# The context's loads, norm and modulation, moved from behind the q projections to ahead of the last GLU pair

## The chip, the cores and the metric

One core of one Trainium2 chip runs the whole program in one launch. The metric is the time of one execution on the device in microseconds; the median of several runs is compared. The core has five engines that run side by side, each with its own list of instructions that it takes in order: TensorE (matmuls, PE), VectorE (DVE), ScalarE (ACT), GpSimd (POOL) and SyncE (SP), which here issues the DMA transfers. They wait for each other by semaphores.

## The reference

The program computes two blocks on 512 tokens of width 1024, in float32. The change lies in the first, a mixer with attention and convolution that is conditioned on a vector `c` and on a context of 256 tokens:

```python
mod = silu(c) @ w_mod + b_mod;          shift, scale, gate = split(mod, 3)
mod_c = silu(c_ctx) @ w_mod + b_mod;    shift_c, scale_c, gate_c = split(mod_c, 3)
u  = rms_norm(x,   norm_w) * (1 + scale)   + shift
uc = rms_norm(ctx, norm_w) * (1 + scale_c) + shift_c
p = u @ w_in                            # columns: q, k, v, za, GLU (a and g), zc
q, k, v = heads of p; q and k rms-normed per head, then rotated by position
k_c, v_c = heads of uc @ w_in[:, k and v columns]; k_c rms-normed
attn = softmax(q @ [k_c; k].T / 8) @ [v_c; v] * silu(za)
conv = pointwise(silu(layer_norm(depthwise_conv31(a * sigmoid(g))))) * silu(zc)
h = x + gate * (concat(attn, conv) @ w_out)
```

So the context enters in one place: its normed and modulated rows `uc` are multiplied with the key and value columns, and give 256 further keys and values. The second block (a delta-rule recurrence, attention to a memory, a feed-forward layer) follows on `h` and is not touched.

## The kernel before, in words

**Numbers.** Every large matmul is done in three passes: each operand is split into a high part (a rounded copy, by ScalarE) and a low part (the difference, by VectorE), and `mm3` adds high x high, high x low and low x high. A weight slab of 128 x 1024 therefore costs a DMA into `wr` (two buffers), a cast into `wh` on ScalarE (three buffers) and a subtraction into `wl` on VectorE (two buffers). `Weights` hands slabs out in a fixed list: two of the last GLU pair, four of q, two of k and v, then the gates and the output. It loads one ahead.

**Order.** The kernel is written as one stream, and a planner orders each engine's instructions from it: among those that are ready in its own model the earliest written goes first. Two things bind it. A tag such as `pj` is a pool of so many buffers, and a new tile waits for an old one's last reader. And `wrote` (line 71) adds an order among the tiles of one tag: the first write of a tile comes after the first write of the tile allocated before it. The convolution's steps are written with a priority 1500 places later (`LATER`), so that they fill what VectorE has free.

**The stages of block 1** (`block1`, from line 338). First the x rows are loaded and normed. A loop over eight column tiles `j` multiplies them with three pairs of GLU columns, in six accumulators; on the way it computes the modulation in groups (`mod_pair`), whose weights are four loads of 512 KB each into the tag `modw` (ten buffers), issued two groups ahead: groups 4 and 5, for the gate, at `j` = 4 and 6. Then come, in the order of writing: three `glu`, the two gate groups (`mod_gate`, each a product in `pj`, a copy to `tA`, small products in `pv`), constants, the emission of convolutions 0 to 2 (`conv`), the last GLU pair (`proj` into `pj` and `pv`, then `glu` and `conv(3)`), the q projections in four weight slabs into the two buffers of `s`, and the k and v projections of six tiles of 128 tokens, in the order 2 to 5 (own tokens) and 0, 1 (context). Then follow rotary, gates, scores and values.

**The context's work.** Two loads of 512 KB bring its eight column tiles (`cxs`, in `modw`). `norm_bs` squares them on ScalarE, adds them up on VectorE one after the other (`SumSq`, in `tA`, four buffers), sums over the partitions on TensorE into `pj` (one buffer), takes the root on ScalarE, spreads the result by two transposes into `pv` (one buffer) and copies it to `modw`. `apply_mod` then takes, for each of eight tiles, a product, a scaling and a subtraction on VectorE and one activation on ScalarE. Before, the loads are written behind the first q slab and the norm behind the third (`CTX = (0, 2)`), and the modulation behind the k and v weights. The `tA` and `pj` of the last GLU pair are thus written ahead of those of the context.

Of the kernel before, what the change touches and what calls it, by code (L numbers as in the profile page):

```python
# [12 lines left out]
F32R = mybir.dt.float32r  # L13
# [12 lines left out]
KT = 8  # L26
# [120 lines left out]
def rest(k, src, hi, lo):  # L147
    return k.V.tensor_tensor(out=lo, in0=src, in1=hi.bitcast(F32), op=ALU.subtract)
# [32 lines left out]
def mm3(k, ps, wh, wl, ah, al, first, last):  # L181
    mm = k.T.matmul
    mm(ps, wh, ah, start=first, stop=False)
    mm(ps, wh, al, start=False, stop=False)
    k.mm = mm(ps, wl, ah, start=False, stop=last)
    return k.mm


def proj(k, ps, w, acts, order=None, tick=None):
    wh, wl = w  # L190
    order = list(order or range(len(acts)))
    for i, kt in enumerate(order):
        c = slice(kt * P, (kt + 1) * P)
        r = mm3(k, ps, wh[:, c], wl[:, c], acts[kt][0], acts[kt][1], i == 0, i == len(order) - 1)
        if tick:
            tick(r, 3)
# [67 lines left out]
def bcast(k, r, n, tag):  # L264
    b = k.t(tag)
    for j in range(n):
        k.T.transpose(b[:, j * P:(j + 1) * P], r[:, j:j + 1].to_broadcast([P, P]), k.ident)
    return b
# [64 lines left out]

MODW = 10
LATER = 1500
CTX = (0, 2)
WARM = 12
ZG = (1, 0, 1, 1, 1, 0, 0, 0, 0, 0, 0)

def block1(k, I, st, h1d):  # L340
    A, V, T, G, Y = k.A, k.V, k.T, k.G, k.Y
# [33 lines left out]
    def mod_load(g, i):  # L375
        t = k.t("modw", [2, S])
        Y.dma_start(out=t, in_=I["w_mod"][g, i])
        return t
# [14 lines left out]
    def mod_pair(g, ts, e0=0, e1=2):  # L393
        cols = mod_group(ts, e0, e1)
        for e in range(e0, e1):
            j = 2 * g + e
            V.tensor_scalar(out=shift[:, :, j], in0=cols[:, 2 * e, :], scalar1=k.vec("b_mod", j), scalar2=None, op0=ALU.add)
            V.tensor_scalar(out=A1[:, :, j], in0=cols[:, 2 * e + 1, :], scalar1=bm1[:, j:j + 1],
                            scalar2=k.vec("norm_w", j), op0=ALU.add, op1=ALU.mult)
# [5 lines left out]
    def norm_bs(vals, w, tag):  # L405
        ss = SumSq(k, "tA", w)
        for v in vals:
            ss.add(v)
        r = ss.rstd("pj", k.inv1k, 1e-6, k.cal([w // P]))
        b = bcast(k, r, w // P, "pv")  # L410
        bs = k.t(tag, [D] if tag == "modw" else [w])[:, :w]
        mark[1] = A.activation(bs, b[:, :w], AF.Copy)
        return bs

    def apply_mod(x, w, bs, i, j, hi, lo, vec=False):
        t = k.t("tA", [w])
        mark[1] = V.tensor_tensor(out=t, in0=x, in1=bs, op=ALU.mult)
        a_ap, s_ap = A1[:, i, j:j + 1], shift[:, i, j:j + 1]
        A.activation(hi, t, AF.Identity, bias=s_ap, scale=a_ap)
        if vec:  # L420
            V.tensor_scalar(out=t, in0=t, scalar1=a_ap, scalar2=s_ap, op0=ALU.mult, op1=ALU.add)
        else:
            mark[2] = A.activation(t, t, AF.Identity, bias=s_ap, scale=a_ap)
        V.tensor_tensor(out=lo, in0=t, in1=hi.bitcast(F32), op=ALU.subtract)
        return hi, lo
# [17 lines left out]
    def half_load(e):  # L443
        for i in range(4):
            Y.dma_start(out=mods[0][i][:, :, e * 256:(e + 1) * 256], in_=I["w_mod"][0, i][:, :, e * 256:(e + 1) * 256])
    half_load(0)
    raws = []

    def raw_load(j):
        raw = k.t("wr", [1024])  # L450
        Y.dma_start(out=raw[:, :768], in_=I["w_start"][j])
        raws.append(raw)
# [5 lines left out]
    for j in range(KT):  # L458
        raw, wh, wl = raws[j], k.t("wh", [1024], F32R), k.t("wl", [1024], F32R)
        A.activation(wh[:, :768], raw[:, :768], AF.Copy)  # L460
        if j < 2:
            mod_pair(0, mods[0], j, j + 1)
        elif j % 2 == 0:
            mod_pair(j // 2, mods[j // 2])
        u = apply_mod(xs[j], S, bs, 0, j, k.t("U", dt=F32R), k.t("U", dt=F32R))
        us.append(u)
        rest(k, raw[:, :768], wh[:, :768], wl[:, :768])
        if j + 2 < KT:
            raw_load(j + 2)
        if j % 2 == 0 and j // 2 + 2 < 6:  # L470
            mods.append([mod_load(j // 2 + 2, i) for i in range(4)])
        for m in range(6):
            c = slice(m * P, (m + 1) * P)
            mm3(k, accs[m], wh[:, c], wl[:, c], u[0], u[1], j == 0, j == KT - 1)
# [12 lines left out]
    def conv(i):  # L487
        u, cw = up[i], lambda w: k.cw[:, i * 31 + w:i * 31 + w + 1]
        y = ys[i] = k.t("hg")
        A.activation(y, u, AF.Identity, scale=cw(15), bias=k.vec("conv_b", i))  # L490
        with k.tc.high_priority(offset=-LATER):
            for w in range(31):
                if w != 15:
                    o0, o1 = max(0, 15 - w), min(S, S + 15 - w)
                    V.scalar_tensor_tensor(out=y[:, o0:o1], in0=u[:, o0 + w - 15:o1 + w - 15], scalar=cw(w), in1=y[:, o0:o1],
                                           op0=ALU.mult, op1=ALU.add)
# [10 lines left out]
    k.rest()  # L507
    for i in range(3):
        conv(i)
    pa, pg = k.t("pj"), k.t("pv")  # L510
    proj(k, pa, W1.next(), us)
    proj(k, pg, W1.next(), us)
# [4 lines left out]
    for g in range(4):  # L517
        wh, wl = W1.next()
        for kk in range(2):
            j = 2 * g + kk  # L520
            c = slice(kk * S, (kk + 1) * S)
            for t in range(4):
                tt = slice(t * P, (t + 1) * P)
                uh, ul = us[j]
                ps = q_ps[t // 2][:, t % 2, :]
                T.matmul(ps, uh[:, tt], wh[:, c], start=j == 0, stop=False)
                T.matmul(ps, uh[:, tt], wl[:, c], start=False, stop=False)
                T.matmul(ps, ul[:, tt], wh[:, c], start=False, stop=j == KT - 1)
        if g == CTX[0]:
            cxs = []  # L530
            for j in range(2):
                c2 = k.t("modw", [4, 256])
                Y.dma_start(out=c2, in_=I["ctxT"][:, 4 * j:4 * j + 4, :])
                cxs += [c2[:, i, :] for i in range(4)]
        if g == CTX[1]:
            cbs = norm_bs(cxs, 256, "modw")
    kw = [W1.next(), W1.next()]
    cus = []
    for j in range(KT):
        if j % 4 == 0:  # L540
            ch, cl = k.t("modw", [4, 256], F32R), k.t("modw", [4, 256], F32R)
        cus.append(apply_mod(cxs[j], 256, cbs, 1, j, ch[:, j % 4, :], cl[:, j % 4, :], True))
    kvs = [None] * 6
    for t in (2, 3, 4, 5, 0, 1):
        ps = k.t("pt", [256])
# [227 lines left out]
    for pr in range(4):  # L773
        for half in range(2):
            i = 2 * pr + half
# [706 lines left out]
def emit(tc, I, out, dbg=None, stages=("b1", "b2", "ff")):  # L1482
    k = K(tc, dbg)
    nc = tc.nc
    with ExitStack() as st:
        k.open(st, "g", dict(g=1, wr=2, wh=3, wl=2))
        setup(k, I)
        h1d = nc.dram_tensor("h1d", (KT, P, S), F32, kind="Internal").ap()
        k.open(st, "H", dict(xa=6, xb=4, hg=16))
        p1 = ExitStack()  # L1490
        k.open(p1, "p1", dict(c1=1, U=16, tA=4, kvs=6))
        k.open(p1, "p1m", dict(pj=1), PSUM)
        k.open(p1, "p1s", dict(s=2), PSUM)
        k.open(p1, "p1t", dict(pt=2), PSUM)
        k.open(p1, "p1v", dict(pv=1), PSUM)
        if "b1" not in stages:
            k.rest()
        if "b1" in stages:
            nm = block1(k, I, p1, h1d)
        else:  # L1500
            nm = Norm(k, "norm_mix_g", "hg", "xb")
            for j in range(KT):
                x = k.x()
                k.Y.dma_start(out=x, in_=I["xT"][:, j, :])
                k.Y.dma_start(out=h1d[j], in_=x)
                nm.add(j, x)
        p1.close()
        k.nx = 0
        if "b2" in stages:
            k.open(st, "p2a", dict(c2=1, p=6, rk=4, v=2, z=2, bon=3, s8=6, nr=8))  # L1510
            k.open(st, "p2m", dict(pj=2), PSUM)
            k.consts("c2", 1350)
            block2(k, I, nm, h1d, out)
# [95 lines left out]
```

## Time and profile before

| | |
|---|---|
| runs shown | 1123.86, 1128.74, 1131.17 us (median 1128.74) |
| profiled execution | 1126.26 us |
| its span, first to last instruction | 1124.5 us |
| mean granted TensorE clock | 0.988 of full |
| TensorE busy | 1076.2 us, 96% |
| VectorE busy | 726.4 us, 65% |
| ScalarE busy | 537.6 us, 48% |
| GpSimd busy | 67.5 us, 6% |
| HBM read and written | 91.24 and 4.19 MB, 85 GB/s over the span |

The span is what the trace covers; the execution's own time is a little longer. Busy times are sums over one engine and say little about waits: an engine that is idle costs nothing unless another, on the path that sets the end, waits for it. The page's chain of work that ended last follows the waits back from the end. For a change in one stage, the busy time of each engine in that stage and its timeline are read. A row of a timeline merges like instructions that follow each other; its length is that of all of them. All operations are recorded through one helper, so every row has line L57, and groups are told apart by the names of their tiles. `hg<-hg,c` on VectorE is a convolution step, `tA<-tA` one of the adds, `wl<-wr,wh` a weight split.

### The profile page before, as it was taken

What the parts mean: (1) busy time and instruction counts of PE and PEld (TensorE: products, weight loads), DVE (VectorE), ACT (ScalarE), POOL (GpSimd) and SP (SyncE); (2) the same over time, 40 slices, a digit from 0 to 9 for tenths busy, and PEclk for the clock granted to TensorE, in tenths of its full rate; (3) what the DMA queues carried; (4) which work ended last, traced back from release to release, by engine and by line L of the source; (5) the groups of instructions that cost most, each with busy time, mean ns of one, the idle gap of its engine ahead of it and who ended that gap; (6) DMA issues with size and microseconds to landing.
All of it is one profiled execution on the core that took longest, in us unless ns stands there. A gap on an engine that the chain in (4) does not pass through costs nothing.

```text
span 1124.5 us, 15949 instructions
## 1 busy us (share of the span) xinstructions
PE 1076.2 (96%) x6272; PEld 832.4 (74%) x6272; DVE 726.4 (65%) x1253; ACT 537.6 (48%) x987; POOL 67.5 (6%) x223
## 2 busy tenths in 40 slices
PE   8999989999988999999999898999999999999998
PEld 4668866666766777777678666768888888888887
DVE  3379999995674898797867777666444344334332
ACT  5445546775554555465555565556433233134210
POOL 0000000000021102121211121010000000000000
PEclk9999999999998999999999899999999999999999
DMA  9752221010352101101012122122332223332232
GB/s 340 280 182 94 75 75 38 1 38 20 119 188 75 57 20 38 37 21 39 20 38 71 48 66 76 38 64 87 107 100 94 94 94 96 105 99 94 94 122 85
DMA packets 32203, 96.46 MB, mean 86 GB/s; under 512 B 3456, under 2 KB 6272, under 8 KB 32128
## 3 DMA queue, kind: packets, MB, share of 16 engines
q1 hardware_dynamic: 32128, 95.45, 25.8%
q8 instruction: 49, 0.80, 0.3%
q14 instruction: 26, 0.21, 0.1%
HBM read 91.24 MB, written 4.19 MB: 85 GB/s over the span
## 4 chain that ended last, share of the span: by engine, by line
PE 83%; DVE 5%; ACT 4%; POOL 3%; DMA 3%; issue 2%; SPq 0%; ACTq 0%; DVEq 0%; POOLq 0%
PE pf L57 31%; PE pj L57 22%; PE s L57 9%; PE i L57 7%; PE pt L57 6%; PE pv L57 5%; PE y L57 3%; POOL nr L57 3%; DMA modw<-w_mod 1%; ACT p L57 1%; DMA wr<-w_start 1%; DVE wl L57 1%; DVE hg L57 1%; ACT wh L57 1%; ACT xb L57 1%
## 5 line engine op out<-in xcount | busy, mean ns | idle before, releaser
L57 ACT ACTIVATE wh<-wr 128x1024 fp32r<-128x1024 f32 (+1 forms) x132 | 137.6, 1042 | 185.5 <-PE pf L57 75.1
L57 DVE TENSOR_TENSOR wl<-wr,wh 128x1024 fp32r<-128x1024 f32 (+1 forms) x132 | 158.8, 1204 | 24.7 <-PE pt L57 10.2
L57 PE MATMUL pj<-hg,wh 128*128 128x512 f32 x448 | 155.0, 418 | 3.9 <-ACT wh L57 1.8
L57 PE MATMUL pf<-A,wh 128*128 128x512 f32 x512 | 157.8, 389 | 0.0
L57 ACT ACTIVATE f<-i 128x512 f16<-128x512 f32 (+1 forms) x132 | 71.9, 597 | 89.0 <-PE i L57 88.6
L57 PEld LDWEIGHTS pf<-A,wh 128*128 128x128 f32 x512 | 95.9, 188 | 19.8
L57 PE MATMUL pf<-A,wl 128*128 128x512 f32 x256 | 99.6, 389 | 0.0
L57 PEld LDWEIGHTS pj<-hg,wh 128*128 128x128 f32 x448 | 81.3, 193 | 21.7 <-ACT wh L57 2.2
L57 DVE TENSOR_TENSOR x<-x,pf 128x512 f32<-128x512 f32 (+1 forms) x33 | 22.2, 671 | 113.9 <-PE pf L57 113.9
L57 PE MATMUL pj<-hg,wl 128*128 128x512 f32 x224 | 90.9, 406 | 0.9 <-DVE wl L57 0.9
L57 DVE SCALAR_TENSOR_TENSOR hg<-hg,c 128x499 f32<-128x499 f32 (+14 forms) x120 | 84.8, 737 | 0.7 <-ACT hg L57 0.4
L57 PE MATMUL pf<-ff,wh 128*128 128x512 f32 (+1 forms) x272 | 79.6, 377 | 0.0
L57 PE MATMUL pf<-hg,wh 128*128 128x512 f32 x256 | 78.8, 389 | 0.0
L57 DVE SCALAR_TENSOR_TENSOR fr<-pf,r 128x512 f32<-128x512 f32 x32 | 22.1, 691 | 85.4 <-PE pf L57 82.1
L57 ACT ACTIVATE fr<-fr 128x512 f32<-128x512 f32 x32 | 20.2, 632 | 99.9 <-DVE fr L57 99.9
L57 PEld LDWEIGHTS <-f 128*128 128x128 f16 x720 | 46.0, 100 | 23.7 <-issue 14.7
L57 PE MATMUL i<-f 128*128 128x128 f16 x672 | 55.6, 224 | 5.6 <-DVE f L57 5.0
L57 PEld LDWEIGHTS pf<-ff,wh 128*128 128x128 f32 x272 | 50.1, 188 | 9.4
L57 PEld LDWEIGHTS pf<-A,wl 128*128 128x128 f32 x256 | 48.1, 188 | 10.1
L57 PEld LDWEIGHTS pf<-hg,wh 128*128 128x128 f32 x256 | 48.0, 188 | 9.9
L57 PE MATMUL pf<-ff,wl 128*128 128x512 f32 (+1 forms) x136 | 51.2, 376 | 0.0
L57 PEld LDWEIGHTS pj<-hg,wl 128*128 128x128 f32 x224 | 42.9, 192 | 9.8 <-DVE wl L57 1.3
(307 smaller groups left out, 2120.6 us busy)
## 6 DMA issues: line engine op xcount, KB each, us to landing
wr<-w_ff SPq DMA_DIRECT2D x64, 512.0 KB, 3.5
modw<-w_mod SPq DMA_DIRECT2D x20, 512.0 KB, 7.3
wr<-rw_in SPq DMA_DIRECT2D x20, 512.0 KB, 3.5
wr<-w_in SPq DMA_DIRECT2D x10, 512.0 KB, 3.6
wr<-w_out SPq DMA_DIRECT2D x8, 512.0 KB, 3.6
wr<-w_start SPq DMA_DIRECT2D x8, 384.0 KB, 5.8
x<-xT SPq DMA_DIRECT2D x8, 256.0 KB, 5.2
modw<-w_mod SPq DMA_DIRECT2D x8, 256.0 KB, 6.4
```

What stands on the lines that cost most here:

```text
L57: r = f(*a, **kw)
```

## The change

The two context loads are issued in the loop over column tiles, at `j` = 5, behind the load of the last start weights and ahead of group 5's four loads. The norm and the modulation are written behind the emission of convolutions 0 to 2 and ahead of the last GLU pair. The same instructions are issued, with the same operands; `CTX` goes.

```diff
--- before.py
+++ after.py
@@ -333,7 +333,6 @@
 
 MODW = 10
 LATER = 1500
-CTX = (0, 2)
 WARM = 12
 ZG = (1, 0, 1, 1, 1, 0, 0, 0, 0, 0, 0)
 
@@ -444,7 +443,7 @@
         for i in range(4):
             Y.dma_start(out=mods[0][i][:, :, e * 256:(e + 1) * 256], in_=I["w_mod"][0, i][:, :, e * 256:(e + 1) * 256])
     half_load(0)
-    raws = []
+    raws, cxs = [], []
 
     def raw_load(j):
         raw = k.t("wr", [1024])
@@ -469,6 +468,11 @@
             raw_load(j + 2)
         if j % 2 == 0 and j // 2 + 2 < 6:
             mods.append([mod_load(j // 2 + 2, i) for i in range(4)])
+        if j == 5:
+            for i in range(2):
+                c2 = k.t("modw", [4, 256])
+                Y.dma_start(out=c2, in_=I["ctxT"][:, 4 * i:4 * i + 4, :])
+                cxs += [c2[:, e, :] for e in range(4)]
         for m in range(6):
             c = slice(m * P, (m + 1) * P)
             mm3(k, accs[m], wh[:, c], wl[:, c], u[0], u[1], j == 0, j == KT - 1)
@@ -507,6 +511,12 @@
     k.rest()
     for i in range(3):
         conv(i)
+    cbs = norm_bs(cxs, 256, "modw")
+    cus = []
+    for j in range(KT):
+        if j % 4 == 0:
+            ch, cl = k.t("modw", [4, 256], F32R), k.t("modw", [4, 256], F32R)
+        cus.append(apply_mod(cxs[j], 256, cbs, 1, j, ch[:, j % 4, :], cl[:, j % 4, :], True))
     pa, pg = k.t("pj"), k.t("pv")
     proj(k, pa, W1.next(), us)
     proj(k, pg, W1.next(), us)
@@ -526,20 +536,7 @@
                 T.matmul(ps, uh[:, tt], wh[:, c], start=j == 0, stop=False)
                 T.matmul(ps, uh[:, tt], wl[:, c], start=False, stop=False)
                 T.matmul(ps, ul[:, tt], wh[:, c], start=False, stop=j == KT - 1)
-        if g == CTX[0]:
-            cxs = []
-            for j in range(2):
-                c2 = k.t("modw", [4, 256])
-                Y.dma_start(out=c2, in_=I["ctxT"][:, 4 * j:4 * j + 4, :])
-                cxs += [c2[:, i, :] for i in range(4)]
-        if g == CTX[1]:
-            cbs = norm_bs(cxs, 256, "modw")
     kw = [W1.next(), W1.next()]
-    cus = []
-    for j in range(KT):
-        if j % 4 == 0:
-            ch, cl = k.t("modw", [4, 256], F32R), k.t("modw", [4, 256], F32R)
-        cus.append(apply_mod(cxs[j], 256, cbs, 1, j, ch[:, j % 4, :], cl[:, j % 4, :], True))
     kvs = [None] * 6
     for t in (2, 3, 4, 5, 0, 1):
         ps = k.t("pt", [256])
```

## Rows read from the trace of the kernel before

**Rows 1.** the page, chain that ended last, share of the span by engine
```profile
PE 83%; DVE 5%; ACT 4%; POOL 3%; DMA 3%; issue 2%; SPq 0%; ACTq 0%; DVEq 0%; POOLq 0%
```

**Rows 2.** stretches: length, busy PE PEld DVE ACT POOL (instructions), clock, DMA share, GB/s
```profile
56.00:73.50 17.50, 15.36 (x89) 9.79 (x89) 9.44 (x19) 12.14 (x16) 0.00 (x0) 1.00 0.78 267
73.50:145.80 72.30, 72.30 (x391) 62.83 (x391) 71.76 (x152) 32.70 (x61) 0.00 (x0) 1.00 0.25 81
145.80:166.30 20.50, 16.65 (x77) 12.98 (x76) 19.52 (x39) 10.89 (x24) 0.00 (x0) 0.92 0.22 64
166.30:266.50 100.20, 94.17 (x604) 64.25 (x603) 84.24 (x147) 67.98 (x129) 0.00 (x0) 1.00 0.09 30
```

**Rows 3.** timeline of VectorE: start, length, engine, line, operation, tiles, shapes, count
```profile
258.15 0.69 DVE L57 SCALAR_TENSOR_TENSOR hg<-hg,c 128x497 f32<-128x497 f32 x1
```

**Rows 4.** timeline of TensorE, 69 to 270 us
```profile
69.89 1.92 PE L57 MATMUL pj<-modw,c 128*32 128x512 f32 x16
...
73.51 0.71 PE L57 MATMUL pj<-U,wh 128*128 128x512 f32 x2
...
100.35 0.50 PE L57 MATMUL pj<-g,tA 128*128 128x1 f32 x4
...
153.72 1.22 PE L57 MATMUL pj<-U,wh 128*128 128x512 f32 x2 [2.51 <-DVE hg L57]
...
266.33 3.60 PE L57 MATMUL pj<-hg,c 128*128 128x512 f32 x8
```

**Rows 5.** timeline of ScalarE, 60 to 104 us
```profile
60.78 1.04 ACT L57 ACTIVATE wh<-wr 128x1024 fp32r<-128x1024 f32 x1
...
64.98 0.60 ACT L57 ACTIVATE tA<-s 128x512 f32<-128x512 f32 x1 [1.85 <-PE s L57]
...
71.94 0.60 ACT L57 ACTIVATE tA<-pj 128x512 f32<-128x512 f32 x1 [0.74 <-PE pj L57]
72.44 0.80 ACT L57 ACTIVATE hg<-hg,g,c 128x512 f32<-128x512 f32 x1
...
85.47 0.58 ACT L57 ACTIVATE tA<-pv 128x512 f32<-128x512 f32 x1
85.94 1.02 ACT L57 ACTIVATE tA<-modw 128x256 f32<-128x256 f32 x3
...
101.62 1.28 ACT L57 ACT_TABLE_LOAD   x1
102.92 0.26 ACT L57 ACTIVATE c<-pj,g 128x2 f32<-128x2 f32 x1
```

**Rows 6.** timeline of SyncE's queue: DMA issues
```profile
45.46 0.33 SPq L57 DMA_DIRECT2D wr<-w_start  x1
45.88 8.48 SPq L57 DMA_DIRECT2D modw<-w_mod  x4
...
65.38 0.35 SPq L57 DMA_DIRECT2D modw<-ctxT  x1
```

**Rows 7.** timeline of VectorE, 86 to 95 us
```profile
86.69 0.42 DVE L57 TENSOR_TENSOR tA<-tA 128x256 f32<-128x256 f32 x1
87.03 0.73 DVE L57 SCALAR_TENSOR_TENSOR hg<-hg,c 128x502 f32<-128x502 f32 x1
...
93.77 0.42 DVE L57 TENSOR_TENSOR tA<-tA 128x256 f32<-128x256 f32 x1
```

**Rows 8.** stretch behind an idle TensorE, columns as in Rows 2
```profile
153.40:156.80 3.40, 3.08 (x7) 2.49 (x8) 3.40 (x10) 2.23 (x8) 0.00 (x0) 0.50 0.47 154
```

**Rows 9.** stretch of the last start loads
```profile
45.00:50.00 5.00, 5.00 (x24) 4.14 (x23) 1.39 (x2) 0.20 (x1) 0.00 (x0) 1.00 0.99 344
```

**Rows 10.** VectorE's groups in attention: shapes, count, busy us, mean ns, idle before
```profile
L57 DVE SCALAR_TENSOR_TENSOR hg<-hg,c 128x505 f32<-128x505 f32 (+14 forms) x59 | 42.4, 735 | 0.2
```

**Rows 11.** DMA issues from 45.4 to 45.8 us: count, KB, us to landing
```profile
wr<-w_start SPq DMA_DIRECT2D x1, 384.0 KB, 8.3
```

**Rows 12.** stretch, VectorE instructions on tile tA alone: length, busy us (count), clock
```profile
84.50:114.50 30.00, 11.68 (x32) 1.00 0.27 88
```

## The prediction

> **What bounds the kernel now.** I began with the chain of the page: TensorE holds 83% of it [rows 1], so a step costs time only where it makes TensorE wait, and saves time only where TensorE waits today. The table of stages shows where that is [rows 2]. From 73.5 to 145.8 us (last GLU pair, q, kv, first gates) TensorE is busy 72.3 us of 72.3: no wait to win back. From 145.8 to 166.3 it is busy 16.65 of 20.5, from 166.3 to 266.5 (attention) 94.17 of 100.2. VectorE is almost full from 73.5 on too, but the convolution fills its gaps there; the last step of that ends near 258.8, and its reader starts at 266.33 [rows 3, 4]. So the context's work is hidden today, beside matmuls that need nothing of it before the last two kv tiles.
>
> Then I read the stretch into which the step moves. Group 5 of the modulation is multiplied at 69.89; the last GLU pair's first matmul into `pj` follows at 73.51 [rows 4]. The copy that frees `pj` for it starts on ScalarE at 71.94 [rows 5].
>
> **The norm, and the wait that it makes.** `pj` has one buffer, and `wrote` keeps the slots of a tag in program order. Before, the order of `pj` is group 4, group 5, GLU pair, context sums. After, the context's sums stand ahead of the GLU pair, which cannot start until the square root has read them. The scratch `tA` goes by program order as well, so the squares cannot start before group 5's copy. The trace shows that this rule bites: the second context load is issued at 65.38, yet the squares start at 85.94, right behind the last GLU's `tA` at 85.47 [rows 5, 6].
>
> The chain, link by link:
> - Group 5's copy and the third convolution's opening step end at 72.44 + 0.80 = 73.24. Three squares take 1.02, so 0.34 each; the second ends near 73.9 [rows 5].
> - Seven dependent adds on VectorE. Today a convolution step follows each: an add starts at 86.69, the step at 87.03, the last add at 93.77 [rows 7]. An add and a step make 0.34 + 0.66 = 1.0. Convolutions 0 to 2 are emitted by then in the new order too, so I keep the pattern: the last add starts at 73.9 + 6 x 1.0 = 79.9 and ends at 80.3.
> - Four sums on TensorE take 0.50 [rows 4], the square root 0.26 [rows 5], and three hand-overs 0.1 each, as from 69.89 + 1.92 = 71.81 to 71.94: 81.4. The table load (1.28 [rows 5]) lies under the adds, behind eight squares that end at about 76.
>
> So the pair starts at 81.4 in place of 73.51: **+7.9 us**. Nothing fills the hole: the q projection's second matmul needs a `wl` slot that the pair holds. Low end: adds back to back, 7 x 0.42 = 2.9, a hole of 4.4. High end: as long as the row, 86.69 to 94.2 with a weight split among the adds, 9.0.
>
> The Trainium skill's page Perfetto Trace Analysis (Optimizing Tensor Performance, Matmuls) says that independent matmul groups should rotate through different PSUM banks, so that one's evacuation overlaps the next's matmuls. Had these two groups a bank each, the hole would be zero and the sum lower by hole and clock; the rows show one `pj`, and decide.
>
> **Clock.** The pair at 153.72 waited 2.51 us for VectorE, and the granted clock from 153.4 to 156.8 was 0.50, 1.2 GHz [rows 4, 8]. A hole of 7.9 us should do the same: some 3.1 us of work at half pace, **+1.6**. Low end 0 (the slow stretch falls into the hole), high end twice, 3.2.
>
> **Loads.** Each context load is 512 KB. Before, they go out behind the GLU's and q's weights, the second at 65.38. After, they stand behind the last start weights (45.46) and ahead of group 5 (45.88) [rows 6]: on SyncE's queue they pass group 5's four loads, two constants and the weights up to the first of q. Nothing on GpSimd moves. Today two loads of group 5 leave at 45.88 at once, and the four take 8.48 us because the others wait for slots of group 3. The context takes those two places, so until 54 the bytes in flight are the same; after that 1 MB more stands in front of the last GLU weights, at 344 GB/s [rows 9] 3.0 us. Group 5 lands some 8 us before 69.89 even so: nothing. The cast of those weights moves from 60.78 to about 63.1, and with it the first GLU's tanh from 64.98 to 63.1 + 1.0 + 1.3 = 65.4 [rows 5]: **+0.4**, ends 0 and 1.
>
> **Modulation.** Eight rounds of three VectorE steps move to about 83 to 92, beside the pair's matmuls. TensorE reads the result only in the last two kv tiles: nothing, or up to 1 if the first q weights' split queues behind it.
>
> **What comes back.** VectorE runs on in the hole: about 9 us / 0.66 = 14 convolution steps get done early. They go missing from attention, where 59 steps [rows 10] lie beside 6.0 us of idle TensorE: 14/59 of 6.0, 1.4, at the very best. I take **-0.5**. The stall at 145.8 to 166.3 stays, since the rotary steps and the reciprocal root ahead of the scores follow the last kv tile, which shifts with the rest.
>
> **Sum:** 7.9 + 1.6 + 0.4 - 0.5 = +9.4 us. The profiled execution took 1126.26 (span 1124.5), so 1135.7 by it. It lies 2.5 below the median of the runs shown (1128.74); on their mean, 1127.9, the sum gives **1137**. A difference of 1% (11.3 us) is about what a measurement of this kernel can tell from no change; the forecast stays just inside.
>
> **Rivals.**
> - *Slower by over 1%: the start weights wait too.* The load at 45.46 took 8.3 us [rows 11] behind four modulation loads, and its cast, near 53.8, stands ahead of group 3's copy on ScalarE. The context's loads wait for no slot; the start weights wait for a split. If the planner issues the context first, they land 3.0 us later, and the modulation of the last columns with them: +12.4, 1140. Against it: group 5's first loads were as free and were not put ahead. It decides if that cast starts past 55. The doubled clock loss alone gives 1139, both 1142.
> - *Faster: VectorE is the true bound.* The context's 31 steps on VectorE, 11.7 us with one other [rows 12], leave the full stretch. Put where VectorE is busy 9.44 of 17.5 us (56 to 73.5), they would let gates and scores come earlier. Ceiling: the idle of the two later stages, 3.85 + 6.0, and 1.6 of slow clock, so -11.4 and 1116. It needs the squares well before 72, which the order of `tA` forbids.
> - *The move is nominal.* If the adds and sums fell into idle time without holding the pair, nothing would change: 1126 to 1129. The order of `pj` speaks against it.
>
> **Chances.** Forecast (+4 to +11) 0.60; start weights or double clock (+11.3 to +16) 0.27; nominal 0.09; VectorE relief 0.04, of which 0.03 over 1%. Some of the forecast's own upper end lies over the bound as well (0.07), so: faster 0.03, within 1% 0.63, slower 0.34. Range 1129 to 1145: from a hole at its low end with little clock loss on the lowest run shown, to both mishaps with the spread of the runs.
>
> **What would show it.** In the trace after: TensorE idle for 4 to 9 us ahead of the last GLU pair, released by ScalarE's square root; squares right behind group 5's copy; adds alternating with convolution steps; a granted clock of 0.50 behind the hole; q, kv and the first scores 8 to 10 us later; the convolution done well ahead of its reader. The prediction is wrong if the pair starts before 76, if the last start weights' cast starts past 55, or if the shift at the first scores is not the shift at the end.

## The result, and the profile after

| | before | changed kernel |
|---|---|---|
| median of runs | 1129.95 us (4 runs) | 1141.74 us (4 runs, 1140.14 to 1143.07) |
| ratio to before, 95% interval | | 1.0114, 1.0081 to 1.0147 |
| span of the profiled execution | 1124.5 us | 1141.3 us |
| mean granted TensorE clock | 0.988 | 0.975 |

The change made the kernel slower by about 1.1%. The forecast was 1137 us, just inside 1%; the time came out 4.7 us higher, inside the range (1129 to 1145), and just outside the bound. Run again beside other kernels (`e0_after` below), the change took 1142.02 us, ratio 1.0119.

The table of stages of the changed kernel, cut where [rows 2] are cut, but with the hole in front of the last GLU pair as a row of its own:

```profile
56.00:74.25 18.25, 15.78 (x84) 9.46 (x84) 8.59 (x18) 10.24 (x14) 0.00 (x0) 0.92 0.71 256
74.25:85.79 11.54, 4.08 (x14) 3.21 (x15) 9.33 (x22) 6.44 (x13) 0.00 (x0) 0.50 0.07 27
85.79:158.00 72.21, 72.21 (x375) 62.35 (x376) 70.05 (x139) 28.86 (x50) 0.00 (x0) 0.96 0.24 74
158.00:180.00 22.00, 17.52 (x85) 13.50 (x84) 21.75 (x46) 10.92 (x24) 0.00 (x0) 1.00 0.25 75
180.00:281.20 101.20, 94.46 (x607) 64.36 (x605) 76.48 (x133) 67.97 (x130) 0.00 (x0) 1.00 0.10 31
```

In the second row TensorE is busy 4.08 of 11.54 us, at a clock of 0.50. The stretch that was full before (third row) is as full, and starts 12.3 us later. But its clock is 0.96, and the row ends short of the same work. The gate product into `pj` that stands ahead of the stall of [rows 4] starts at 145.61 before, 72.1 us behind the pair:

```profile
145.61 0.62 PE L57 MATMUL pj<-U,wh 128*128 128x512 f32 x2
```

In the changed kernel it starts at 160.22, 74.4 us behind the pair, so the stretch is also 2.3 us longer. The timeline of TensorE (as [rows 4]) shows this row, and what stands in the hole:

```profile
70.65 3.15 PE L57 MATMUL pj<-modw,c 128*32 128x512 f32 x16
74.55 1.87 PE L57 MATMUL pv<-g,tA 128*128 128x2 f32 x8 [0.76 <-ACT tA L57]
77.93 1.22 PE L57 MATMUL s<-wh,U 128*128 128x512 f32 x2 [1.51 <-ACT wh L57]
84.45 0.99 PE L57 MATMUL pj<-g,tA 128*128 128x1 f32 x4 [5.30 <-DVE tA L57]
85.79 0.80 PE L57 MATMUL pj<-U,wh 128*128 128x512 f32 x1 [0.35 <-ACT c L57]
...
160.22 0.62 PE L57 MATMUL pj<-U,wh 128*128 128x512 f32 x2
...
168.55 0.73 PE L57 MATMUL pj<-U,wh 128*128 128x512 f32 x2 [2.73 <-DVE hg L57]
...
281.24 1.13 PE L57 MATMUL pj<-hg,c 128*128 128x512 f32 x2
```

The pair's first matmul is released by ScalarE's square root (`c`), 0.35 us before; the four sums in front of it waited 5.30 us for VectorE's adds. The first two matmuls of q slip in ahead, and no more. ScalarE's timeline (as [rows 5]):

```profile
73.90 0.60 ACT L57 ACTIVATE tA<-pj 128x512 f32<-128x512 f32 x1 [1.95 <-PE pj L57]
74.39 0.80 ACT L57 ACTIVATE hg<-hg,g,c 128x512 f32<-128x512 f32 x1
75.10 1.02 ACT L57 ACTIVATE tA<-modw 128x256 f32<-128x256 f32 x3
...
81.82 1.28 ACT L57 ACT_TABLE_LOAD   x1
85.47 0.26 ACT L57 ACTIVATE c<-pj,g 128x2 f32<-128x2 f32 x1 [2.37 <-PE pj L57]
```

The squares stand right behind group 5's copy and the convolution's opening step, and the table load lies under the adds. VectorE's timeline (as [rows 7], the last row as [rows 3]):

```profile
76.46 0.16 DVE L57 TENSOR_TENSOR c<-pv,g 128x4 f32<-128x4 f32 x1 [3.56 <-PE pv L57]
...
77.34 0.73 DVE L57 SCALAR_TENSOR_TENSOR hg<-hg,c 128x497 f32<-128x497 f32 x1
77.99 0.42 DVE L57 TENSOR_TENSOR tA<-tA 128x256 f32<-128x256 f32 x1
78.32 0.73 DVE L57 SCALAR_TENSOR_TENSOR hg<-hg,c 128x497 f32<-128x497 f32 x1
78.97 0.42 DVE L57 TENSOR_TENSOR tA<-tA 128x256 f32<-128x256 f32 x1
...
83.89 0.41 DVE L57 TENSOR_TENSOR tA<-tA 128x256 f32<-128x256 f32 x1
...
250.12 0.74 DVE L57 SCALAR_TENSOR_TENSOR hg<-hg,c 128x497 f32<-128x497 f32 x1
```

Adds alternate with convolution steps, 0.98 us each. But the first add does not follow the second square (done near 75.8): VectorE first stands idle for 3.56 us in front of group 5's own add (`c<-pv,g`), which waits for TensorE's small products, then does four constants and a convolution step. The convolution's last step ends near 250.9, 30 us before its reader at 281.24; before it was 7.5 us. Attention (180 to 281.2) has 44 of its steps, for 59 (as [rows 10]):

```profile
L57 DVE SCALAR_TENSOR_TENSOR hg<-hg,c 128x500 f32<-128x500 f32 (+14 forms) x44 | 32.1, 738 | 0.3
```

SyncE's queue (as [rows 6]):

```profile
46.37 0.33 SPq L57 DMA_DIRECT2D wr<-w_start  x1
46.79 1.41 SPq L57 DMA_DIRECT2D modw<-ctxT  x2
54.47 2.81 SPq L57 DMA_DIRECT2D modw<-w_mod  x4
```

The start weights kept their place ahead of the context. The granted clock (as [rows 8]) of the hole and what follows, and of the next stretch:

```profile
71.30:91.70 20.40, 12.48 (x41) 7.97 (x34) 16.84 (x43) 9.91 (x19) 0.00 (x0) 0.50 0.11 33
...
91.70:96.00 4.30, 4.30 (x21) 3.51 (x20) 4.30 (x13) 3.70 (x6) 0.00 (x0) 1.00 0.00 0
```

**How far the shift carries.** Profiles differ by up to 1.5 us ahead of group 5's product (`pj<-modw,c`, 69.89 before; 69.12 to 70.67 over all of them), so I measure from its start. Read off the timelines of TensorE, us behind that start:

| | pair | first q matmul with `wl` | first kv | first scores | block 2's first product |
|---|---|---|---|---|---|
| before | 3.62 | 14.59 | 36.67 | 94.41 | 258.09 |
| change, first profile | 15.14 | 29.18 | 50.49 | 107.65 | 271.64 |
| change, second profile (`e0_after`) | 13.12 | 25.93 | 47.24 | 105.59 | 269.30 |

What is lost at the pair and its two slabs is lost for good: +14.6 and +11.3 at q, +13.6 and +11.2 at block 2. Nothing of it comes back in attention. The two profiles are of executions near either end of their kernel's times: 1143.07 us, the longest of four, and 1138.10, the second shortest of six.

### The profile page after: what moved, and what is told of

It reads as the page before. It is cut to its first block, busy times and chain, and to the rows that moved or that the text cites. A ratio compares the mean times of both kernels' runs of the same rounds, so it can differ in the third digit from the quotient of the medians.

```text
span 1141.3 us, 15952 instructions
## 1 busy us (share of the span) xinstructions
PE 1086.9 (95%) x6272; PEld 839.1 (74%) x6272; DVE 726.7 (64%) x1253; ACT 538.4 (47%) x987; POOL 67.5 (6%) x223
## 4 chain that ended last, share of the span: by engine, by line
PE 82%; DVE 7%; ACT 4%; POOL 3%; issue 2%; DMA 1%; SPq 0%; ACTq 0%; DVEq 0%; POOLq 0%
PE pf L57 31%; PE pj L57 22%; PE s L57 9%; PE i L57 7%; PE pt L57 5%; PE pv L57 4%; PE y L57 3%; POOL nr L57 3%; DVE hg L57 2%; ACT p L57 1%; DVE wl L57 1%; DMA wr<-w_in 1%; ACT xb L57 1%; DVE p L57 1%; ACT tA L57 0%
## 5 line engine op out<-in xcount | busy, mean ns | idle before, releaser
L57 DVE SCALAR_TENSOR_TENSOR hg<-hg,c 128x505 f32<-128x505 f32 (+14 forms) x120 | 84.6, 742 | 0.4
L57 DVE SCALAR_TENSOR_TENSOR fr<-pf,r 128x512 f32<-128x512 f32 x32 | 22.1, 691 | 85.4 <-PE pf L57 82.1
```

Source lines behind the costliest of these rows:

```text
L57: r = f(*a, **kw)
```

## Experiments

The theory: with one buffer `pj` the pair waits for the context's norm, and the slow clock follows. Rivals: the loads that moved up the queue (B), and VectorE's crowding (C). All kernels below are the changed kernel with one edit; ratios are to the kernel before.

**The change again**, without an edit:

> The change itself, beside the kernels that vary it. Theory A as the profile after shows it (pair late by some 11 us, three more in the pair at half clock): ratio 1.009 to 1.014, TensorE idle 5 us or more ahead of the sums, and a granted clock of 0.5 again somewhere between 70 and 92. If the long half clock in the first profile was an accident of that run, the pair's two slabs take near 11 us here and the ratio is nearer 1.009.

1142.02 us, ratio 1.0119 (1.0095 to 1.0143). Its profile had group 5's product at full clock (1.92 us as before), and is the cleaner one to take the sum apart with.

**Another bank for the context's sums and spread.**

```diff
-    def norm_bs(vals, w, tag):
+    def norm_bs(vals, w, tag, pp=("pt", "pt")):
-        r = ss.rstd("pj", k.inv1k, 1e-6, k.cal([w // P]))
-        b = bcast(k, r, w // P, "pv")
+        r = ss.rstd(pp[0], k.inv1k, 1e-6, k.cal([w // P]))
+        b = bcast(k, r, w // P, pp[1])
```

> The change as it is, but the context's sums and their spread use the two buffers of pt, which nobody needs before the kv tiles, in place of pj and pv. Theory A (the single pj makes the last GLU pair wait for the context's norm, and the wait brings the slow clock): the pair starts near 74 as before, no idle ahead of it over 2 us, the whole near the kernel before, ratio 0.998 to 1.004, some 11 to 13 us below the change. Rival B (the context's loads push group 5 and the GLU weights back): stays at the change's time, ratio 1.009 or more. Rival C (the context's steps crowd VectorE and ScalarE ahead of the first q weights' split): the pair starts near 74, but the q projection starts late, ratio 1.004 to 1.008.

1128.81 us, ratio 1.0001 (0.9985 to 1.0017). TensorE's timeline:

```profile
74.38 1.05 PE L57 MATMUL pv<-g,tA 128*128 128x2 f32 x8 [0.76 <-ACT tA L57]
75.30 0.71 PE L57 MATMUL pj<-U,wh 128*128 128x512 f32 x2
```

The pair follows the small products at once, while ScalarE and VectorE do the norm as in the changed kernel (first square at 74.93). Its 1.7 us more than before behind group 5's start come from a granted clock of 0.51 from 70.2 to 73.6 in this profile. The edit also moves the spread off `pv`, so this run alone doesn't part the two; in the trace of the change the pair's first matmul, which writes `pj`, is released by the square root that reads `pj`. So the wait for `pj` carries the loss: loads, adds and modulation are where the change put them, and cost nothing that the interval shows. They also gain nothing, which fells the rival that hoped for relief on VectorE. The Trainium skill's page Perfetto Trace Analysis (Optimizing Tensor Performance, Matmuls), cited in the prediction, wants independent groups in different PSUM banks; this run agrees, at 1.0001 against 1.0114.

**The loads alone**: norm and modulation put back where they stood before.

```diff
-    cbs = norm_bs(cxs, 256, "modw")
-    cus = []
...
+        if g == 2:
+            cbs = norm_bs(cxs, 256, "modw")
     kw = [W1.next(), W1.next()]
+    cus = []
...
```

> Only the loads are moved as in the change; norm and modulation stay where the kernel before has them. Theory A: nothing is lost, ratio 0.998 to 1.003, the pair starts between 73.5 and 74.5. Rival B (loads): most of the loss is here, ratio 1.007 or more, with TensorE waiting for group 5 or for the GLU weights. Rival C says as A here.

1128.66 us, ratio 1.0005 (0.9990 to 1.0021); the pair at 73.30, group 5 at 69.69. Theory B falls. The stall of [rows 4] at 153.72 is longer in this profile, with norm and modulation at their old place (3.39 us for 2.51):

```profile
154.95 1.22 PE L57 MATMUL pj<-U,wh 128*128 128x512 f32 x2 [3.39 <-DVE hg L57]
```

**The norm and the modulation right behind the GLU pair.**

```diff
+    pa, pg = k.t("pj"), k.t("pv")
+    proj(k, pa, W1.next(), us)
+    proj(k, pg, W1.next(), us)
+    glu(pa, pg)
+    conv(3)
     cbs = norm_bs(cxs, 256, "modw")
...
-    pa, pg = k.t("pj"), k.t("pv")
-    proj(k, pa, W1.next(), us)
-    proj(k, pg, W1.next(), us)
-    glu(pa, pg)
-    conv(3)
```

> Loads as in the change; norm and modulation written right behind the last GLU pair, in place of right ahead of it, so that pj and tA go to the pair first. Theory A: the pair starts near 74, the sums run beside the q projection, ratio 0.998 to 1.004. Rival B: as the change, 1.009 or more. Rival C (VectorE crowded early on): between, 1.004 to 1.008.

1130.15 us, ratio 1.0026 (1.0009 to 1.0042). With the pair written first, the hole is gone: the pair starts 4.9 us behind group 5's start, 1.3 more than before, and as much is group 5's own product at a slow clock (3.22 us for 1.92). A rest of some 2.9 us stays in the time. TensorE's stall of [rows 4] at 153.72 is longer:

```profile
157.28 1.22 PE L57 MATMUL pj<-U,wh 128*128 128x512 f32 x2 [3.46 <-DVE hg L57]
```

3.46 us for 2.51. But `e2_loads` has nearly the same stall with norm and modulation at their old place, and `e1_pt` has both early and loses nothing, so this stall does not show VectorE's crowding (C). Where the rest comes from stays open. If it is C, it is a matter of 2.9 us, 4.7 at the end of the interval, not of 12.

**The convolutions 0 to 2 written behind the pair**, so that their steps don't stand between the adds.

```diff
-    for i in range(3):
-        conv(i)
     cbs = norm_bs(cxs, 256, "modw")
...
-    conv(3)
+    for i in range(4):
+        conv(i)
```

> The change, but convolutions 0 to 2 are written behind the last GLU pair, so that no convolution step stands between the context's adds. Theory A with the adds as the length of the hole: seven adds of about 0.45 in place of 0.98 us each and no step ahead of the first one, so the hole is 4 to 5 us shorter, the half clock a little shorter too, and the whole 4 to 7 us below the change, ratio 1.005 to 1.008 to the kernel before; the convolution, late by some 10 us, still ends before its reader. If the convolution is then what ends last before the layer norm, the gain is less, 1.009 or more. Rival B or C: the hole's length changes nothing, 1.010 to 1.013.

1132.71 us, ratio 1.0048 (1.0031 to 1.0066). VectorE's timeline:

```profile
75.28 0.16 DVE L57 TENSOR_TENSOR c<-pv,g 128x4 f32<-128x4 f32 x1 [3.06 <-PE pv L57]
...
75.75 0.42 DVE L57 TENSOR_TENSOR tA<-tA 128x256 f32<-128x256 f32 x1
76.09 0.29 DVE L57 TENSOR_TENSOR kc<-rt,c 128x128 f32<-128x128 f32 x1
76.29 0.42 DVE L57 TENSOR_TENSOR tA<-tA 128x256 f32<-128x256 f32 x1
...
77.36 2.01 DVE L57 TENSOR_TENSOR tA<-tA 128x256 f32<-128x256 f32 x4
80.84 0.17 DVE L57 RECIPROCAL c<-c 128x2 f32<-128x2 f32 x1 [1.46 <-ACT c L57]
```

The adds now come about 0.5 us apart, and the pair starts 10.7 us behind group 5's start, for 13.1 (`e0_after`), although TensorE ran at a granted 0.51 from 70.6 to 74.0 in this profile, under group 5's product. The ratio is 0.0071 below that of `e0_after`, some 8 us, where the intervals allow 3 to 13. The profile accounts for less: block 2 starts 266.19 us behind group 5's start, for 269.30, a gain of 3.1 us, or 4.5 but for the slow group 5 (3.32 us for 1.92). The filler of one chain is the delay of another.

**Seven more dependent steps on VectorE behind the adds** (a product with 1.0).

```diff
             ss.add(v)
+        for _ in range(7):
+            V.tensor_scalar(out=ss.prev[:, :w], in0=ss.prev[:, :w], scalar1=1.0, scalar2=None, op0=ALU.mult)
```

> The change, with seven more dependent VectorE steps of the same width (a product with 1.0) between the context's adds and its sums. Theory A (the adds, each with a convolution step behind it, are the length of the hole, one for one): 7 x 0.98 = 6.9 us more, with no more than 1 us more of half-clock work, ratio 1.016 to 1.019. Rival (something else ends the wait, such as group 5, the loads or the weights' split): less than 3 us more, ratio below 1.014.

In the trace the steps took 0.85 us each with their convolution step, 5.95 in all, and the sums waited for all of it:

```profile
86.87 0.99 PE L57 MATMUL pj<-g,tA 128*128 128x1 f32 x4 [11.01 <-DVE tA L57]
88.21 0.80 PE L57 MATMUL pj<-U,wh 128*128 128x512 f32 x1 [0.35 <-ACT c L57]
```

The pair starts 19.09 us behind group 5's start, 6.0 more than in `e0_after`, and block 2 6.7 more: a step on this chain costs its whole length. The times are weaker evidence: 1142.79 us and 1.0149 (1.0124 to 1.0173), below the 1.016 that I expected at least and above the rival's 1.014; the interval of the change itself reaches to 1.0143, and the profiled execution took 1149.15 us, well above the median. The trace shows the link, the times don't show its size.

**Group 5's own add written behind the seven adds.**

```diff
     def mod_gate(g, ts):
...
-        V.tensor_tensor(out=gate[...], in0=cols[:, :, 0], in1=k.vec("b_mod", 4 * g, 4), op=ALU.add)
+        return lambda: V.tensor_tensor(out=gate[...], in0=cols[:, :, 0], in1=k.vec("b_mod", 4 * g, 4), op=ALU.add)
...
-            ss.add(v)
+            end = ss.add(v)
+        k.after(last(), end)
...
-    for g in (4, 5):
-        mod_gate(g, mods[g])
+    mod_gate(4, mods[4])()
+    last = mod_gate(5, mods[5])
```

> The change, with group 5's own add on VectorE (128x4, it waits for TensorE's small products) put behind the context's seven adds in VectorE's order, where the change has it ahead of them. If the adds wait in the queue behind that add: the first one starts with its second square, at about 76 in place of 78, the pair 1.5 to 2 us earlier, ratio lower by 0.0015 to 0.002 than the change's. Rival (the adds wait for their squares or for the convolution step only): no difference, pair at the same distance behind the squares.

1139.33 us, ratio 1.0112 (1.0092 to 1.0132): 0.0007 below `e0_after`, for the 0.0015 to 0.002 that I expected, and not to be told from it. The trace is clearer. VectorE's timeline:

```profile
74.02 0.43 DVE L57 TENSOR_TENSOR tA<-tA 128x256 f32<-128x256 f32 x1 [1.19 <-ACT tA L57]
```

The squares start at 73.27, and the first add is now released by the second of them, 0.75 us behind; in `e0_after` it is 2.07 (73.47 to 75.54), in the first profile 2.89. So the place behind group 5's add, with the constants and the convolution step that stood between, cost 1.3 to 2.1 us of the hole. In this profile most of the gain was lost again to a slow group 5 (2.84 us for 1.92): the pair starts 12.71 us behind group 5's start, for 13.12.

**Fillers in the hole.** Matmuls that nobody reads keep TensorE at work, to see what the clock costs.

```diff
             ss.add(v)
+        fl = k.t("pt")
+        for _ in range(28):
+            T.matmul(fl, us[0][0][:, 0:P], us[0][0], start=True, stop=True)
```

> The change, with 28 matmuls of 512 columns into a free buffer of pt, whose result nobody reads, written between the context's squares and its sums: TensorE works while it waits. Theory A with a clock term: granted clock 1.00 all through, group 5 takes 1.9 us, the pair's two slabs 11 in place of 14 us, and the whole lies 3 to 6 us below the change, ratio 1.005 to 1.009. Rival (the clock costs next to nothing, since it is slow where TensorE has nothing to do): as the change, or later by what the fillers put in front of group 5, ratio 1.010 or more.

1144.07 us, ratio 1.0137 (1.0116 to 1.0159): a miss, with the rival's ratio (1.010 or more), and the pair's slabs took 13.34 us, not 11. The fillers, and two matmuls of q behind them, ended 2.47 us ahead of the sums, and the clock fell just where the pair stood (stretch in the pair):

```profile
85.10:88.50 3.40, 3.40 (x10) 2.65 (x9) 3.40 (x11) 2.11 (x5) 0.00 (x0) 0.53 0.00 0
```

With 42 in place of 28:

> The changed kernel with 42 filler matmuls in place of 28, written ahead of the context's sums, into a buffer of pt that nobody reads; the rest is unchanged. With 28 the fillers ended 2.47 us before the sums and the pair's slabs still ran at half clock (7.90 us for the slab into pj, where the kernel before takes 5.53 at full clock). 28 fillers took about 6.2 us, so 42 end at the sums or less than 1 us behind them. If the clock's term is real and comes from TensorE standing idle: both slabs of the pair at full clock, 11.0 to 11.2 us from the pair's first matmul to q's, against 12.8 to 14.0 in the changed kernel; the pair itself starts where it did or up to 0.5 us later; the whole 1.5 to 3 us below the changed kernel, a ratio of 1.009 to 1.011. Rival, the half clock does not come from the hole: the slabs take 12.8 us or more again, and the ratio is 1.012 to 1.014 as in the changed kernel and with 28 fillers.

1139.16 us, ratio 1.0091 (1.0075 to 1.0107). TensorE's timeline and the clock over hole and pair:

```profile
73.94 8.23 PE L57 MATMUL pt<-U 128*128 128x512 f32 x35
82.00 0.50 PE L57 MATMUL pj<-g,tA 128*128 128x1 f32 x4
...
82.92 0.68 PE L57 MATMUL pj<-U,wh 128*128 128x512 f32 x2
...
84.49 0.43 PE L57 MATMUL pv<-g,c 128*128 128x128 f32 x2 [0.45 <-DVE c L57]
```

```profile
74.00:95.00 21.00, 20.55 (x93) 16.56 (x93) 20.89 (x50) 11.79 (x22) 0.00 (x0) 1.00 0.07 27
```

Now the clock stays at full speed, the sums take 0.50 in place of 0.99, and q starts 24.54 us behind group 5's start, for 25.93 and 29.18 in the two profiles of the change. The pair itself starts as late as ever (12.67): the hole stays, its echo goes. All five profiles with an unfilled hole in front of the pair (the two of the change, `e4_noconv`, `e6_double`, `e7_defer`) have a clock of 0.50 where the pair starts, this one 1.00. So here the slow clock around the pair did come from the hole. One expectation failed: the slabs took 11.87 us, not 11.0 to 11.2, because the context's spread (`pv<-g,c`) now stands among the pair's matmuls and waits 0.45 us for VectorE. In time that is worth about 3 us (1.0091 against 1.0119), with intervals that overlap; in the profile the gain at q is gone by block 2 (269.92 us behind group 5's start, for 269.30), after other slow stretches on the way (a clock of 0.59 from 240 to 244).

## Why the prediction held, and where it did not

- **The wait for `pj`:** right, link by link, and `e1_pt` shows it to be the cause. Its size was too small, and this is the step that failed: "the second ends near 73.9" and the first add at once. I took the pace of the adds from [rows 7] rightly (1.0; it was 0.98), but not what already stands in VectorE's queue at that place: group 5's own add, which waits for TensorE, then constants and one convolution step. That is 1.3 us in `e0_after`. The sums at half clock add 0.5. With 7.9 this makes 9.7; measured there are 9.5 (13.12 less 3.62), and 11.5 in the first profile, where group 5 itself ran at half clock for another 1.2 and its small products for 0.8 (1.87 us for 1.05).
- **The clock:** the pair's two slabs took 10.97 us before, 12.81 in `e0_after` and 14.04 in the first profile: +1.8 and +3.1, where I took 1.6 with an end at 3.2. In size the first profile is near the rival of the doubled clock loss, the second near the forecast; which one an execution meets was not predictable from the trace of before. But not all of it is the clock, and this I had put at nothing: the context's spread stands among the pair's matmuls, and with a clock of 1.00 the slabs still took 11.87 us (`e8_fill42`). Against that the slow clock cost 0.9 and 2.2. Nor does each such wait bring a slow clock: the stall that I took the term from was followed by 0.50 [rows 8], the same stall in the first profile (2.73 us, up to 168.55) by 1.00 (fourth row of its table).
- **Loads:** 0 instead of 0.4 (`e2_loads`). The start weights waited for nothing new (their cast starts at 53.98 in the first profile, 53.83 before), so that rival did not happen. And the cast that I had ahead of the first GLU's tanh was put behind it: the tanh starts at 65.81, the cast at 66.30.
- **What comes back:** 0 instead of -0.5. The convolution did get done early, and as I counted: attention has 15 steps fewer, for my 14, and the last ends 30 us ahead of its reader, for 7.5. But attention did not get shorter: from the first scores to block 2 TensorE needs as long as before (163.7 us in `e0_after` and before). So the part of TensorE's idle time that I credited was not the convolution's doing. The q stage (first q matmul to first kv) gave back 0.8 in exchange, 21.3 us for 22.1, as the context's sums and spread left it for the pair's slabs.
- **The sum:** 9.5 + 1.8 - 0.8, some 0.7 more on the way to the scores, makes the 11.2 of `e0_after` at block 2, for a forecast of 9.4. Of the first profile's 16.8 us of longer span, 0.8 lie ahead of group 5, 13.6 up to block 2, and the rest behind it, where TensorE ran at 0.51 from 528.7 to 535.5 and the second profile at 1.00; I can't tie that to the change. By my own sign this profile speaks against the prediction: its shift at the first scores, 13.2, is not the one at the end, 16.0. In `e0_after` they are 11.2 and 11.5.
- **Which side of 1%** hung on 2 us: the forecast of 9.4 lay inside the 11.3 that make 1%; measured is 1.1%, with an interval that reaches below 1%. Of the 4.7 us between forecast and time about 2.0 lie in the kernel before, whose four runs have a median of 1129.95 where I started from 1127.9, and 2.4 in the change (11.8 for 9.4); the rest is rounding.

**Open:** why the clock falls at one place in one execution of a kernel and at another in the next, and hence how the medians divide between hole and clock.

## What to carry to other kernels

Before a step is moved ahead of another, look at which single-buffered accumulator they share: in a program whose buffers go round in the order of writing, the earlier one's whole chain of small dependent steps then stands in front of the later one's matmuls. Cost such a chain from the engine's queue at the new place, with what already stands there and waits, not from the duration of its links at the old place. And a step that is hidden beside full matmuls may be at its best place already; here moving it gained nothing even once the wait was gone.

## What the runs showed that I had not expected

- Half-clock time depends on the execution as much as on the kernel: the same code had 20.4 us at 0.50 around the hole in one profile and 10.2 us (76.2 to 86.4, at 0.51) in another.
- With 28 fillers TensorE's idle time ahead of the sums was down to 2.47 us, and the pair still met a clock of 0.53. Filling a part of the idle stretch took the slow clock out of the hole, but not off the pair behind it.
- VectorE's convolution steps of 0.73 us between dependent adds doubled the length of the chain (0.98 an add, against some 0.5 without them), though they are written with a priority 1500 places later: the order of VectorE has a step behind each add, and the next add stands behind it.
